# An encoder layer: the FFN's second operand split before it is turned, and three weight blocks visited one sequence at a time

## The chip, the cores and the metric

The kernel runs on one core of a Trainium2 chip. The metric is the device time of one execution in microseconds (us); with several runs, their median. The engines of the core work side by side and in order, each on its own list: TensorE (PE, with its weight loads PEld), VectorE (DVE), ScalarE (ACT), GpSimd (POOL), and SyncE (SP), which issues the DMAs.

## The reference

One encoder layer is applied to two sequences of 1024 positions with 1024 channels, in float32. Cut to what matters:

```python
def encoder_layer(x, ...):
    h = rms_norm(x, norm1)
    proj = h @ w_in                                   # q, k, v, gu, gv
    a = rms_norm(windowed_gqa(q, k, v, ...), attn_out_gain)
    g = rms_norm(chunked_spatial_gating(gu, gv, ...), gmlp_out_gain)
    x = x + jnp.concatenate([a, g], axis=-1) @ w_o    # called x1 below
    h2 = rms_norm(x, norm2)
    return x + (jax.nn.silu(h2 @ w_gate) * (h2 @ w_up)) @ w_down   # D_FF = 2816
```

`rms_norm(x, g)` is `x * rsqrt(mean(x*x) + 1e-6) * g` over the channels.

## The kernel before, in words

Positions are cut into 16 tiles of 128, tiles 0 to 7 for the first sequence (s = 0) and 8 to 15 for the second (s = 1). The kernel goes through these stages: input projections and attention, the gating branch, the output projection with the residual (which gives x1), the gate and up products of the FFN, and the down product.

**Precision.** Every float32 operand of a large product is split into two f16 parts, `hi` (a rounded copy, made by ACT) and `lo` (the rest, made by DVE). A product is then three f16 matmuls into the same PSUM tile: hi by hi, hi by lo, lo by hi.

**Seven products instead of eight.** From the output projection on, a matrix product is done by 2 x 2 blocks with seven block products. Both operands need some sums and differences of their blocks first (four on each side), and the outputs need a few additions behind.

**The FFN's matrices.** Gate and up have 22 column blocks of 128; two of them form a weight block `p`, so there are 11. One "matrix" is the gate (m = 0) or up (m = 1) product of one weight block with one sequence: `matrix(n)` issues seven products of 4 x 3 matmuls of 128x512 (`product`, lines 1895 to 1905). The weights stand still in TensorE (`op`), the sequence's normalised x1 streams past (`tops[s, i]`, seven operands `i`, each with its hi and lo). Between the products `prep(i)` works ahead: it loads the raw weights of the next matrices (`load_raw`), takes their sum of squares (`key_sum`, `key_scale`, which has a small matmul on line 1840) and splits the seven weight operands (`prep_comb`, `prep_hi`, `prep_lo`, lines 1856 to 1886). The list `visits` says which weight block is prepared when and for which sequences; prepared once, it serves all sequences of that visit:

```python
visits = [(0, (0,))] + [(p, (0, 1)) for p in range(1, NP)] + [(0, (1,))]
```

So block 0 is prepared twice, blocks 1 to 10 once, in 12 visits; with gate and up and the sequences there are 44 matrices.

**How the second operand is made.** Behind each pair of position tiles of the output projection, `x1_norm` stores x1, takes the sum of squares (`x1_sq`, ACT) and scales it in place (`x1_scale`, ACT, line 1715). `h2_turn` (line 1723) turns the tile by eight 128x128 transposes on TensorE into PSUM; `h2_out` (line 1730, ACT, eight copies) brings them back with norm2's gain as a scale per partition. `h2_comb` (lines 1751 to 1757, DVE) makes the four block combinations. For s = 0 four of the seven operands are split at once (`part_hi`, `part_lo`, lines 1797 and 1802); everything else is stored in float32 to the scratch tensors `t_d`, loaded again (`top_load`) and split in halves of 128x1024 (`top_hi`, `top_lo`, lines 1783 and 1788), for s = 1 between the products of the first matrices (`top_step`).

**What sets the order.** The part from the first load to the preparation of the first weight block is written as steps in a list `steps`. The table `WHEN` holds a number for each step, by its function's name and count; `plan_order` sorts by it, and the sorted list is the order on every engine. All DMAs are issued from SP, in that same order, so a DMA that waits for its data holds up all DMAs behind it. From the first FFN matrix on, instructions stand in the order in which the functions call them.

**The start.** `warm_mm` runs eight matmuls on zeros while the first weights are on their way.

**On-chip memory.** Work tiles of 4 KB per partition come from pools with a fixed number of slots: L 12, M 8, XL 3, XN 3, S 9.

Of the kernel before, what the change touches and what calls it, by code (L numbers as in the profile page):

```python
# [16 lines left out]
P = 128  # L17
# [3 lines left out]
TS = 8  # L21
# [29 lines left out]
        0,  # L51
    ],
    "warm_mm": [
        62,
    ],
    "x0_load": [
        80, 160, 320, 584, 407, 496, 983, 894,
    ],
    "wq_load": [
        40, 0, 240, 200, 673, 762, 1337, 1482,  # L60
    ],
    "x0_hi": [
        516, 693, 1003, 1269, 1092, 1180, 1679, 1590,
    ],
    "x0_lo": [
        598, 775, 1094, 1351, 1174, 1262, 1792, 1672,
    ],
    "wq_hi": [
        427, 339, 870, 932, 1508, 1446, 2226, 2606,
    ],  # L70
    "wq_lo": [
        520, 431, 963, 1029, 1604, 1539, 2319, 2714,
    ],
    "q0": [
        598, 688, 779, 869, 960, 1103, 1194, 1284, 1375, 1465, 1666, 1757, 1848, 1938, 2082, 2172, 2262, 2380, 2470,
        2560, 2651, 2795, 2965, 3065,
    ],
    "gram": [
        520, 546, 1050, 1077, 2028, 2055, 2353, 2742, 2768, 2781, 2885, 2898, 2912, 2925, 2938, 2952,
    ],  # L80
    "row_load": [
        280, 850,
    ],
    "row_mm": [
        1556,
    ],
    "row_out": [
        1732,
    ],
    "row_store": [  # L90
        1821,
    ],
    "wkv_load": [
        1426, 1570,
    ],
    "wkv_hi": [
        2380, 2300, 2810, 2340, 2667, 2525, 2565, 2851,
    ],
    "wkv_lo": [
        2463, 2385, 2882, 2424, 2780, 2819, 2675, 2922,  # L100
    ],
    "gram_sum": [
        3001,
    ],
    "scale_mm": [
        3055, 7203, 23284, 27506,
    ],
    "scale_add": [
        3102, 7528, 23577, 27552,
    ],  # L110
    "scale_pow": [
        3137, 7584, 23612, 27608,
    ],
    "scale_out": [
        3216, 7664, 23692, 27758,
    ],
    "xn_load": [
        1955, 2088, 1072, 1160, 1249, 4141, 6313, 6903, 8320, 9739, 8574, 11961, 15526, 16895, 20520, 22171,
    ],
    "xn_sum": [  # L120
        2707, 2893, 1812, 1945, 2123, 4685, 6864, 7390, 9651, 12184, 11081, 13532, 16276, 17599, 21121, 22809,
    ],
    "xn_eps": [
        2858, 3037, 2865, 2088, 2267, 4891, 7008, 7556, 9797, 12349, 11290, 13718, 16455, 17742, 21265, 22998,
    ],
    "xn_pow": [
        2893, 3072, 2950, 2123, 2302, 5125, 7108, 7640, 9944, 12384, 11325, 13787, 16490, 17777, 21300, 23032,
    ],
    "kv_mm": [
        3156, 3300, 3730, 3957, 4183, 4327, 3443, 3587, 5853, 6062, 6712, 6860, 8416, 8548, 9722, 9854, 12936, 13111,  # L130
        14723, 14984, 15788, 15946, 17320, 17782, 19792, 19923, 22049, 22192, 24192, 24722, 26585, 26716,
    ],
    "q_out": [
        3307, 3192, 3250, 3966, 6460, 8204, 9248, 11570, 12703, 15642, 17702, 18943, 21842, 23660, 25252, 26508,
    ],
    "v_gain": [
        3341, 4036, 3347, 4332,
    ],
    "k_out": [
        3691, 4166, 4558, 4216, 6238, 7720, 8864, 10390, 13304, 15166, 16113, 18110, 20224, 22359, 25188, 27522,  # L140
    ],
    "v_hi": [
        3818, 4191, 4532, 4467, 6967, 7042, 8715, 10021, 13971, 15151, 16128, 17961, 20096, 22374, 24949, 26884,
    ],
    "v_lo": [
        3944, 4260, 4650, 4578, 7015, 7088, 9132, 10074, 14022, 15197, 16727, 18757, 20255, 22518, 25087, 27026,
    ],
    "qk_sq": [
        3756, 4241, 4623, 4303, 6666, 8323, 9517, 11726, 13350, 15720, 18048, 20298, 21949, 24146, 25329, 27635,
    ],  # L150
    "qk_sum": [
        3849, 4338, 4796, 5018, 6774, 8445, 9609, 11832, 13453, 15812, 18209, 20391, 22042, 24243, 25422, 27820,
    ],
    "qk_pow": [
        4667, 4462, 4920, 5181, 6903, 8574, 9739, 11961, 13582, 15942, 18338, 20520, 22171, 24372, 25551, 27949,
    ],
    "qk_scale": [
        4898, 4723, 5160, 5491, 7175, 8811, 10001, 12275, 13841, 16287, 18593, 20748, 22399, 24600, 25779, 28589,
    ],
    "k_turn": [  # L160
        5328, 5087, 5262, 6701, 7277, 9350, 10517, 14310, 13943, 17451, 19502, 22181, 24323, 26891, 28153, 29807,
# [175 lines left out]
        10357,  # L337
    ],
    "vg_load": [
        120,  # L340
    ],
    "ws_sum": [
        16966,
# [2229 lines left out]
```

## Time and profile before

| | |
|---|---|
| median of 3 runs | 1814.62 us (1811.51 to 1817.87) |
| profiled execution, its own time | 1818.09 us |
| its span, from first to last instruction | 1815.8 us |
| mean granted clock of TensorE | 0.995 |
| instructions in the span | 26756 |
| moved by DMA | 298.87 MB, mean 165 GB/s |
| first FFN matmul on line 1900 | 601.8 us after the span's start |
| first down matmul on line 2410 | 1408.9 us |

How to read it: busy time is the time in which an engine had an instruction running; durations hold the latency at an instruction's end, which the next one may overlap. "Idle before, releaser" is the time in which the engine stood before an instruction, and whose end let it go on. The granted clock is the share of full speed that TensorE was given. The DMA share is the mean busy share of the core's 16 DMA engines.

### The profile page before, as it was taken

Reading aid. Unit: us, or ns where it says so; the run is one execution under the profiler, and the core shown is the slowest. Engines: PE = TensorE matmul, PEld = TensorE weight load, DVE = VectorE, ACT = ScalarE, POOL = GpSimd, SP = SyncE. Lnnn points to the kernel's source line nnn. Section 1 sums busy time; section 2 is a strip of 40 time slices with the busy share of each in tenths; the row PEclk is TensorE's granted clock in tenths of the full one; section 3 lists DMA queues with packets and bytes.
Section 4 is the critical chain, followed back from the end, with each engine's and each line's share of the span. In section 5 each row is a group of like instructions: output and inputs, shape, how many; then the busy total and the mean of one; then the engine's idle time right before and its main releaser. Section 6 shows DMA issues by size and latency. Waiting matters only on the chain.

```text
span 1815.8 us, 26756 instructions
## 1 busy us (share of the span) xinstructions
PE 1789.0 (99%) x10046; PEld 880.8 (49%) x10046; DVE 1167.5 (64%) x2180; ACT 1015.0 (56%) x1951; POOL 113.1 (6%) x142
## 2 busy tenths in 40 slices
PE   9899999999999999999999999999999999999999
PEld 7555554554555444444444444444444444444444
DVE  5887577699888886455564564555647846645651
ACT  6887678897878856344453453434534453333340
POOL 1221120031000000000000000000000000000000
PEclk9999999999999999999999999999999999999999
DMA  8599999987767863232331331323353754333641
GB/s 263 146 224 216 236 257 236 263 274 246 243 215 223 287 218 124 76 122 86 117 122 41 122 115 65 111 77 115 111 203 112 270 175 147 87 115 105 231 140 47
DMA packets 247469, 298.87 MB, mean 165 GB/s; under 512 B 136835, under 2 KB 163459, under 8 KB 247340
## 3 DMA queue, kind: packets, MB, share of 16 engines
q1 hardware_dynamic: 247340, 297.17, 54.0%
q8 instruction: 78, 1.28, 0.3%
q14 instruction: 51, 0.42, 0.1%
HBM read 175.46 MB, written 90.19 MB: 146 GB/s over the span
## 4 chain that ended last, share of the span: by engine, by line
PE 84%; DVE 6%; DMA 4%; ACT 3%; issue 2%; POOL 0%; SPq 0%; POOLq 0%; DVEq 0%; ACTq 0%
PE pd L2410 7%; PE pd L2412 7%; PE pd L2411 7%; PE pa L1900 4%; PE pa L1902 4%; PE pa L1901 4%; PE pd L1900 4%; PE pd L1901 4%; PE pd L1902 4%; PE pc L1900 4%; PE pc L1902 4%; PE pc L1901 4%; PE pb L1900 2%; PE pb L1901 2%; PE pb L1902 2%
## 5 line engine op out<-in xcount | busy, mean ns | idle before, releaser
L2410 PE MATMUL pd<-wop,a 128*128 128x512 f16 x616 | 234.2, 380 | 2.1 <-ACT a L718 2.1
L2411 PE MATMUL pd<-wop,a 128*128 128x512 f16 x616 | 234.1, 380 | 0.0
L2412 PE MATMUL pd<-wop,a 128*128 128x512 f16 x616 | 233.9, 380 | 0.0
L1900 PEld LDWEIGHTS <-op 128*128 128x128 f16 x1232 | 122.3, 99 | 142.8
L1902 PEld LDWEIGHTS <-op 128*128 128x128 f16 x1232 | 120.5, 98 | 145.4
L1901 PEld LDWEIGHTS <-op 128*128 128x128 f16 x1232 | 120.5, 98 | 145.5 <-issue 3.4
L1900 PE MATMUL pa<-top,op 128*128 128x512 f16 x352 | 133.4, 379 | 1.3 <-ACT ua L2018 1.2
L1902 PE MATMUL pa<-top,op 128*128 128x512 f16 x352 | 133.4, 379 | 0.0
L1901 PE MATMUL pa<-top,op 128*128 128x512 f16 x352 | 133.4, 379 | 0.0
L718 ACT ACTIVATE wop<-wd,wdr_r 128x512 f16<-128x512 f32 x66 | 47.3, 720 | 152.5 <-PE pd L2412 148.5
L718 ACT ACTIVATE a<-as,asr_r 128x512 f16<-128x512 f32 x154 | 102.0, 709 | 35.6 <-DMA as<-act_d 16.2
L2029 ACT COPY ub<-pc 128x512 f32<-128x512 f32 x44 | 25.7, 585 | 161.0 <-PE pc L1902 161.0
L719 DVE SCALAR_TENSOR_TENSOR a<-as,asr_r,a 128x512 f16<-128x512 f32 x154 | 109.2, 747 | 9.5 <-ACT a L718 9.5
L719 DVE SCALAR_TENSOR_TENSOR wop<-wd,wdr_r,wop 128x512 f16<-128x512 f32 x66 | 49.2, 749 | 98.8 <-ACT wop L718 98.8
L2410 PEld LDWEIGHTS <-a 128*128 128x128 f16 x616 | 60.5, 98 | 75.4 <-ACT a L718 2.6
L2412 PEld LDWEIGHTS <-a 128*128 128x128 f16 x616 | 60.4, 98 | 73.5 <-issue 0.8
L2411 PEld LDWEIGHTS <-a 128*128 128x128 f16 x616 | 60.4, 98 | 72.7 <-issue 0.8
L1828 ACT ACTIVATE junk_e<-g 128x1024 f32<-128x1024 f32 x44 | 46.4, 1054 | 72.4 <-DVE g L2013 72.3
L1277 ACT ACTIVATE sc<-sc,mx 128x384 f32<-128x384 f32 (+1 forms) x128 | 74.3, 582 | 17.8 <-DVE mx L1261 17.5
L2035 DVE TENSOR_TENSOR ub<-ub,ua 128x512 f32<-128x512 f32 x44 | 30.5, 692 | 82.5 <-ACT ub L2029 82.5
L2010 ACT ACTIVATE g<-g,rs 128x512 f32<-128x512 f32 x57 | 41.1, 722 | 62.5 <-DVE g L2045 35.5
L1261 DVE CUSTOM_DVE_ANT_0 sc<-ps,bias 128x384 f32<-128x384 f32 (+1 forms) x128 | 62.2, 518 | 21.4 <-PE ps L1250 15.4
(413 smaller groups left out, 4417.4 us busy)
## 6 DMA issues: line engine op xcount, KB each, us to landing
as<-act_d SPq DMA_DIRECT2D x77, 512.0 KB, 3.7
act_d<-g SPq DMA_DIRECT2D x66, 256.0 KB, 2.0
raw<-in_wg_dram SPq DMA_DIRECT2D x24, 512.0 KB, 4.0
raw<-in_wu_dram SPq DMA_DIRECT2D x24, 512.0 KB, 4.5
act_d<-sa SPq DMA_DIRECT2D x44, 256.0 KB, 2.6
act_d<-sb SPq DMA_DIRECT2D x44, 256.0 KB, 2.2
wds<-in_wd_dram SPq DMA_DIRECT2D x22, 512.0 KB, 3.9
wd<-in_wd_dram SPq DMA_DIRECT2D x22, 512.0 KB, 5.4
```

Of the source, the lines that this page charges most:

```text
L718: nc.scalar.mul(hi, src, gain)
L719: nc.vector.scalar_tensor_tensor(lo, src, gain, hi, ALU.mult, ALU.subtract)
L1261: nc.vector.tensor_tensor_reduce(out=T["sc", t, hp][:, v, :W], in0=T["ps", t, hp][v][:, :W], in1=bias[:, h, off : off + W], scale=1.0, sca ...
L1277: nc.scalar.activation(sc, sc, AF.Exp, bias=T["mn", t][:, h : h + 1], scale=-1.0, accum_out=T["sum", t][:, h : h + 1])
L1828: nc.scalar.activation(junk_e[0], src, AF.Square, accum_out=acc)
L1900: nc.tensor.matmul(ps, op[:, 0, k, :], th[:, k, :], start=first and k == 0, stop=False, **more)
L1901: nc.tensor.matmul(ps, op[:, 0, k, :], tl[:, k, :], start=False, stop=False, **more)
L1902: nc.tensor.matmul(ps, op[:, 1, k, :], th[:, k, :], start=False, stop=last and k == 3, **more)
L2010: nc.scalar.activation(dst, src, AF.Silu, scale=iv)
L2410: nc.tensor.matmul(ps, a[:, 0, s, cs], wop[:, 0], start=first and n == 0, stop=False, **kw)
L2411: nc.tensor.matmul(ps, a[:, 0, s, cs], wop[:, 1], start=False, stop=False, **kw)
L2412: nc.tensor.matmul(ps, a[:, 1, s, cs], wop[:, 0], start=False, stop=end, **kw)
```

## The change: what it does

- **Operand of the FFN.** norm2's gain is loaded as a row to all partitions (`n2_load`), and `x1_scale` multiplies by both the tile's scale and that row, on DVE. The block combinations (`h2_comb`), `hi` and `lo` are made in the natural layout, positions on partitions. Then the f16 parts are turned by DMA transposes on SP: for s = 0 operands 0 to 3 straight from the chip's memory (`h2_turn`), operands 4 to 6 by way of scratch tensors `nat_d` (`h2_store`, `top_turn`). The TensorE transposes, `h2_out`, `part_hi`, `part_lo`, `t_d`, `top_load`, `top_hi`, `top_lo` are gone.
- **Second sequence.** Only x1 is stored in the projection stage. It is read again, scaled, combined, split and turned during the first eight matrices (the list `late_list`).
- **Visits.** Blocks 0, 1, 2 first for s = 0 alone, blocks 3 to 10 for both, blocks 0, 1, 2 last for s = 1 alone: 14 visits.
- **Order.** The first eight matrices (`FIRST = 8`) become steps of the ordered list, cut in half products (`d_product` and its companions). `WHEN` has new numbers for all steps, also for those ahead of the FFN. In `matrix(n)`, for the rest, some additions and outputs stand later, and the last two outputs and the stores come behind the first product of the next matrix.
- **Start and memory.** Fourteen warm matmuls instead of eight; one small ACT copy is put right at the start; slots XL 4, XN 4, S 11, with the scratch for dynamic DMAs set to 256.
- Down's `blocks` follow the order of the visits with s = 1, so blocks 3 to 10 come ahead of 0, 1, 2.

The diff, cut to its core:

```diff
-    slots = {"L": 12, "M": 8, "XL": 3, "XN": 3, "S": 9}
+    slots = {"L": 12, "M": 8, "XL": 4, "XN": 4, "S": 11}
...
+    early = cp.tile([P, 1], F32, name="early")
+    nc.scalar.copy(early, nhalf[:, 0:1])
...
-        for _ in range(8):
+        for _ in range(14):
             nc.tensor.matmul(ps, T["warm"][:, 0:P], T["warm"], start=True, stop=True)
...
+    def n2_load():
+        T["n2row"] = k4("XL", "n2row")
+        nc.sync.dma_start(T["n2row"], n2.to_broadcast([P, D]))
...
     def x1_scale(t):
-        nc.scalar.mul(T["x1", t], T["xr", t], T["r1", t])
+        nc.vector.scalar_tensor_tensor(T["x1", t], T["xr", t], T["r1", t], T["n2row"], ALU.mult, ALU.mult)
-    def h2_turn(t, z):
-        pt = T["ph2", t, z] = xx(f"ph{t}_{z}", [P, 4, P])
-        for j in range(4):
-            k = z * 4 + j
-            nc.tensor.transpose(pt[:, j, :], T["x1", t][:, k * P : (k + 1) * P], ident)
...
+    def h2_comb(t, i):
+        a, b = {4: (3, 0), 3: (6, 3), 1: (6, 4), 5: (2, 1)}[i]
+        nc.vector.tensor_sub(h2_block(t, i), h2_block(t, a), h2_block(t, b))
+    def h2_hi(t, i):
+        nc.scalar.copy(h2_pack(t, i // 2)[:, i % 2, 0], h2_block(t, i))
+    def h2_lo(t, i):
+        pk = h2_pack(t, i // 2)[:, i % 2]
+        nc.vector.tensor_sub(pk[:, 1], h2_block(t, i), pk[:, 0])
+    def h2_store(t, j):
+        s, cs = h2_cs(t)
+        n = 1 if j == 3 else 2
+        store(nat_d[s][j][cs, 0:n], h2_pack(t, j)[:, 0:n])
+    def h2_turn(t, j):
...
+        dst = T["top16", s, j].rearrange("p i z k c -> p (i z k) c")[:, :, cs]
+        load(dst, h2_pack(t, j).rearrange("p i z d -> p (i z d)"), transpose=True)
+    def top_turn(s, i, z):
+        load(top_pair(s, i)[z], nat_d[s][i // 2][:, i % 2, z], transpose=True)
+    LATE = (0, 2, 6, 4, 3, 1, 5)
+    def late_load(t):
+        T["x1", t] = k4("XL" if t % TS < 4 else "XN", f"xl{t}")
+        load(T["x1", t], x1_d[t])
+    def late_scale(t):
+        nc.vector.scalar_tensor_tensor(T["x1", t], T["x1", t], T["r1", t], T["n2row"], ALU.mult, ALU.mult)
...
+    def late_turn(t, i):
+        pk = late_pack(t, i)
+        s, cs = h2_cs(t)
+        pair = top_pair(s, i)
+        if i < 4:
+            dst = T["top16", s, i // 2][:, i % 2].rearrange("p z k c -> p (z k) c")[:, :, cs]
+            load(dst, pk.rearrange("p z d -> p (z d)"), transpose=True)
+        else:
+            for z in range(2):
+                load(pair[z][:, :, cs], pk[:, z], transpose=True)
...
-    visits = [(0, (0,))] + [(p, (0, 1)) for p in range(1, NP)] + [(0, (1,))]
+    visits = [(p, (0,)) for p in range(3)] + [(p, (0, 1)) for p in range(3, NP)] + [(p, (1,)) for p in range(3)]
...
+    def late_list():
+        for t in range(TS, TS + 4):
+            for u in (t, t + 4):
+                yield (late_load, u)
+            for u in (t, t + 4):
+                yield (late_scale, u)
+            for i in LATE:
...
+                for fn in (late_hi, late_lo, late_turn):
+                    yield (fn, t, i)
...
+    for n in range(FIRST):
+        v, m, s = mats[n]
+        last_one = v == FIRST // 2 - 1
+        for i in range(7):
+            for part in range(2):
+                add(d_product, n, i, part)
...
+            key = (v, 1) if m == 0 else (v + 1, 0)
+            if not (m and last_one):
...
+                add(prep_hi, key, i)
+                add(prep_lo, key, i)
+            upto = len(late) * (7 * n + i + 1) // (7 * FIRST)
+            for fn, *args in late[nlate:upto]:
+                add(fn, *args)
...
-    for n in range(len(mats)):
+    for n in range(FIRST, len(mats)):
         matrix(n)
```

More of the change, by code (lines that the diff above doesn't have):

```diff
@@ L659 @@
+    "key_sum": [
+        61103, 61770, 64440, 64693, 67963,
+    ],
+    "key_mm": [
+        61372, 62030, 64777, 65046,
+    ],
+    "key_add": [
+        61419, 62107, 64874, 65094,
+    ],
+    "key_pow": [
+        61481, 62169, 64935, 65156,
+    ],
+    "key_out": [
+        61577, 62321, 65087, 65374,
     ],
@@ L686 @@
     vg: bass.AP,
+    n2: bass.AP,
     tab: bass.AP,
@@ L769 @@
     x1_d = [dr.tile([P, D], F32, name=f"x1_d{t}") for t in range(NT)]
-    t_d = [[dr.tile([P, 4, 512], F32, name=f"t_d{s}_{i}") for i in range(7)] for s in range(2)]
+    nat_d = [[dr.tile([512, 2 - j // 3, 2, 512], F16, name=f"nat_d{s}_{j}") for j in range(4)] for s in range(1)]
     act_d = [dr.tile([P, NF // 2, 2, 512], F32, name=f"act_d{i}") for i in range(7)]
@@ L2018, in matrix @@
         nc.scalar.copy(u2, pa)
+        while behind:
+            behind.pop(0)()
         prep(0)
@@ new lines, in d_pre, with d_product @@
+    def d_pre(n, q):
+        if mats[n][1] == 0 and q:
+            return d_out(n, q)
+        return (d_bank(n, "a"), d_tile(n, "a")[:, 1], d_tile(n, "b")[:, 0], d_tile(n, "a")[:, 0])[q]
+    def d_product(n, i, part):
+        key, s, _ = d_info(n)
+        op = wops[key, i]
+        th, tl = tops[s, i]
+        ps = d_bank(n, "abacdcd"[i])
+        first, final = i in (0, 1, 3, 4), part == 1
+        for k in (2 * part, 2 * part + 1):
+            more = dict(skip_group_check=not first)
+            nc.tensor.matmul(ps, op[:, 0, k, :], th[:, k, :], start=first and k == 0, stop=False, **more)
+            nc.tensor.matmul(ps, op[:, 0, k, :], tl[:, k, :], start=False, stop=False, **more)
+            nc.tensor.matmul(ps, op[:, 1, k, :], th[:, k, :], start=False, stop=final and k == 3, **more)
@@ new lines, in d_store, with key_mm @@
+    def d_store(n, i):
+        _, s, p = d_info(n)
+        sa, sb = (T.get(("ds", n, c)) for c in range(2))
+        if i in (0, 2, 5):
+            a = d_out(n, {0: 0, 2: 1, 5: 2}[i])
+        else:
+            a = {1: lambda: sa[:, 1], 3: lambda: sb[:, 0], 4: lambda: sa[:, 0], 6: lambda: sb[:, 1]}[i]()
+        store(act_d[i][:, p, s, :], a)
+    def key_mm(key):
+        T["kp", key] = xx(f"pk{key[0]}_{key[1]}", [P, 2])
+        nc.tensor.matmul(T["kp", key], onec, wsc[key], start=True, stop=True)
@@ new lines, in key_add, with key_pow, key_out @@
+    def key_add(key):
+        tot = small("m", 1)
+        nc.vector.tensor_reduce(tot, T["kp", key], AX.X, ALU.add)
+        e = T["ke", key] = small("den", 2)
+        for j in range(2):
+            nc.vector.tensor_scalar(e[:, j : j + 1], tot, W_NORM**-2, 1e-37, ALU.mult, ALU.add)
+    def key_pow(key):
+        r = T["kr", key] = small(("f", "sums")[key[1]], 2)
+        nc.gpsimd.tensor_tensor(r, T["ke", key], pm, ALU.pow)
+        wsc[key] = r[:, 0:1]
+    def key_out(key):
+        iv = winvs[key] = small(("rs", "v_ms")[key[1]], 1)
+        nc.vector.tensor_mul(iv, T["kr", key][:, 1:2], n2r[:, 1:2])
```

774 lines of the change are left out of this document (419 added, 355 removed), and 179 rows, old and new, of the table WHEN.

## The prediction

> **What bounds the kernel now.** I read first the page's busy times, then its chain of waits, then TensorE's own waits, and last the busy times by stage. The page (busy us, share of the span, instructions) and the engines' shares of the chain that ended last:
>
> ```profile
> PE 1789.0 (99%) x10046; PEld 880.8 (49%) x10046; DVE 1167.5 (64%) x2180; ACT 1015.0 (56%) x1951; POOL 113.1 (6%) x142
> PE 84%; DVE 6%; DMA 4%; ACT 3%; issue 2%; POOL 0%; SPq 0%; POOLq 0%; DVEq 0%; ACTq 0%
> ```
>
> TensorE is busy for 99% of the span and is 84% of the chain. So a matmul taken away is worth its slot, and other engines matter only where TensorE comes to wait for them. The stages (us from:to, length, then busy us and instructions of PE, PEld, DVE, ACT, POOL; then granted clock, DMA share, GB/s):
>
> ```profile
> 0.00:446.20 446.20, 429.32 (x3624) 248.31 (x3625) 333.81 (x839) 354.69 (x804) 83.33 (x100) 0.98 0.92 234
> 446.20:601.70 155.50, 154.76 (x818) 82.99 (x816) 130.87 (x225) 124.47 (x270) 11.65 (x17) 1.00 0.71 234
> 601.70:746.70 145.00, 141.86 (x665) 65.09 (x663) 105.13 (x157) 89.85 (x152) 3.12 (x4) 1.00 0.58 192
> 746.70:891.70 145.00, 145.00 (x679) 66.38 (x678) 78.90 (x133) 66.34 (x112) 2.78 (x4) 1.00 0.29 102
> ```
>
> The second row is the bulk of the output projection, the third as long a stretch as eight FFN matrices take, the fourth the FFN in its steady state. TensorE stands idle 446.2 - 429.3 = 16.9 us before the projection, 0.7 in it, 3.1 in the first FFN stretch, and not at all in the next.
>
> **The transposes that go.** The change takes all TensorE transposes of the normalised x1 out (line 1723). First the groups by line (count, busy us, mean ns, idle before), then four rows of TensorE in order of time (start, us; in brackets the idle before and what ended it):
>
> ```profile
> L1723 PE MATMUL ph<-ident,xs 128*128 128x128 f32 x128 | 18.1, 274 | 1.9 <-ACT xs L1715 1.9
> L1840 PE MATMUL pks<-mx,onec 128*128 128x2 f32 x40 | 5.6, 209 | 0.0
> ```
>
> ```profile
> 463.33 0.38 PE L1665 MATMUL wc<-wo5h,mo 128*128 128x512 f16 x1
> 463.55 0.60 PE L1723 MATMUL ph<-ident,xs 128*128 128x128 f32 x4
> 463.98 0.38 PE L1663 MATMUL wc<-wo5h,mo 128*128 128x512 f16 x1
> ...
> 607.96 2.13 PE L1723 MATMUL ph<-ident,xs 128*128 128x128 f32 x16 [1.48 <-ACT xs L1715]
> ```
>
> The group's 18.1 us counts the latency at the end of each set. What four transposes cost the engine is start to start: 463.98 - 463.55 = 0.43 us, where a 128x512 matmul takes 463.55 - 463.33 = 0.22. So 32 sets x 0.43 = **13.8 us** leave TensorE, 28 of the 32 in the projection, where it never rests and nothing else can hide them. Their 1.9 us of waits for line 1715 go too: no TensorE instruction of the projection waits for the scaled tile any more. **-15.7 us**.
>
> **Two extra visits.** Weight blocks 0, 1 and 2 are prepared twice, before only block 0: 14 visits instead of 12, four more prepared matrices. On TensorE that is the scale sum of line 1840: 20 matrices cost 5.6 us, four more **+1.1 us**. Their 4 MB of loads, 28 splits on each of ACT and DVE, and 16 sums lie beside matmuls; the fourth stage row has DVE at 78.9 and ACT at 66.3 of 145 us. The late single-sequence visits double the preparation per matmul, still under both engines' room; I cost them at nothing there. Without the cover, one matrix's preparation is some 7 us of DVE.
>
> **The start.** Rows of time from the first 10 us, then three stretches of it:
>
> ```profile
> 1.19 3.19 PE L832 MATMUL ps_warm<-warm 128*128 128x512 f16 x8 [1.19 <-DVE warm L827]
> 3.95 1.28 ACT L856 ACT_TABLE_LOAD   x1 [3.95 <-DMA wqr<-in_w_in_dram]
> 6.63 1.43 PE L904 MATMUL gram<-wqt 128*128 128x128 f32 x8 [2.25 <-ACT wqt L856]
> ```
>
> ```profile
> 6.00:8.00 2.00, 1.37 (x9) 1.38 (x10) 1.85 (x3) 1.19 (x2) 0.00 (x0) 0.81 0.91 244
> 8.00:10.00 2.00, 2.00 (x6) 1.61 (x6) 0.30 (x2) 0.72 (x2) 0.00 (x0) 0.50 1.08 353
> 10.00:14.00 4.00, 4.00 (x19) 3.23 (x18) 2.86 (x7) 2.98 (x5) 0.82 (x2) 0.92 1.12 314
> ```
>
> The table load of ACT waits behind the first weights; the new first copy of ACT brings it ahead of them, up to 1.28 us earlier. After the 2.25 us of idle the granted clock falls to 0.50, which costs 0.4 + 1.0 + 0.3 = 1.7 us over these rows. Six more warm matmuls (6 x 0.22 to 6 x 0.40 us) end at about 6 us, so the hole closes. Against a gain of 3.0 stands that the DMA share is already 0.9 to 1.1 here, so later loads may swallow it: bounds 0 and 3.0, I take the middle, **-1.5 us**. [...]
>
> **VectorE in the projection and in the first eight matrices.** The second operand is now split before it is turned, so the subtractions become 56 of 128x512, with 16 scalings of 128x1024, for what now are 16 + 20 splits and 16 ACT scalings. DVE's rows in order of time show what an instruction costs when it is fed:
>
> ```profile
> 617.13 0.69 DVE L1863 TENSOR_TENSOR ss<-raw 128x512 f32<-128x512 f32 x1
> 617.73 0.69 DVE L2023 TENSOR_TENSOR ua<-pb,ua 128x512 f32<-128x512 f32 x1
> ...
> 638.22 0.75 DVE L1886 SCALAR_TENSOR_TENSOR op<-ss,es_er,op 128x512 f16<-128x512 f32 x1
> 638.88 0.75 DVE L1886 SCALAR_TENSOR_TENSOR op<-st,es_er,op 128x512 f16<-128x512 f32 x1
> ...
> 647.53 1.22 DVE L1788 TENSOR_TENSOR top<-tr,top 128x1024 f16<-128x1024 f32 x1
> 648.66 0.69 DVE L2054 TENSOR_TENSOR sa<-g,g 128x512 f32<-128x512 f32 x1
> ```
>
> Start to start 0.60, 0.66 and 1.13 us, less than the durations beside them. A 128x1024 scaling is not in the trace: between 1.13 and 2 x 0.66; I take 1.24, the 1.13 raised by 0.66/0.60. Eight matrices are 672 matmuls x 0.2156 (145.0 us in the fourth stage row holds 8 x 84 of them and the sums) = 144.9 us of TensorE. DVE's work in them: 40 sums x 0.60 + 16 products x 0.66 + 16 output sums x 0.60 + seven weight matrices (49 splits x 0.66 + 28 sums x 0.60) + the late operand (8 x 1.24 + 16 x 0.60 + 28 x 0.60) = 24.0 + 10.6 + 9.6 + 49.1 + 36.3 = 130 us, 90% of the time. By listed durations it would be 147, more than there is. The present stretch holds 105.1 us of DVE and loses 3.1 us of TensorE, 1.5 of them (607.96) in the waits already taken out above. I let the new one lose 4, which is **+2.4 us** over the 1.6 left; bounds -1.6 (no waits) and, by the durations, 147 - 145 + 4 - 1.6 = +4.4.
>
> In the projection DVE loses about 39 rows of 0.69 us and gets 8 scalings and 44 rows: 130.9 - 27 + 41 = 145 listed us against 155.5 - 12.2 = 143.3 of TensorE, by starts (0.60/0.69) about 126. It fits by the starts. ACT loses the 128 copies of line 1730 and the scalings of 1715, so DVE waits less for it. I add nothing here; the other answer is a rival below.
>
> **DMA and SP's queue.** Rows of SP in order of time; issues with the median us to landing; and the one queue in the attention stage (60 to 340 us) and in the steady FFN (packets, MB, share):
>
> ```profile
> 96.90 3.41 SPq L977 DMA_TRANSPOSE xh<-xq  x1
> 102.53 0.34 SPq L980 DMA_DIRECT2D xh_d<-xh  x1
> ```
>
> ```profile
> tr<-t_d SPq DMA_DIRECT2D x20, 512.0 KB, 5.2
> t_d<-hf SPq DMA_DIRECT2D x16, 256.0 KB, 3.2
> t_d<-ta SPq DMA_DIRECT2D x12, 256.0 KB, 3.9
> t_d<-tb SPq DMA_DIRECT2D x12, 256.0 KB, 3.9
> pT<-ph SPq DMA_TRANSPOSE x64, 4.4
> xh<-xq SPq DMA_TRANSPOSE x16, 5.7
> ```
>
> ```profile
> DMA packets 126739, 63.80 MB, mean 228 GB/s; under 512 B 115730, under 2 KB 115730, under 8 KB 126707
> q1 hardware_dynamic: 126707, 63.38, 98.6%
> ```
>
> ```profile
> q1 hardware_dynamic: 6048, 14.68, 28.2%
> ```
>
> The steady queue moves 14.68 MB in 28.2% of 145 us, 359 GB/s. In the attention stage the small packets, 115730 x 256 B = 29.6 MB, are the transposes; the other 33.8 MB take 94 of 276 us, so the transposes run at 163 GB/s, 3.2 us for 512 KB. The change turns 14.7 MB (8 + 6 of 512 KB for the first sequence, 28 blocks of 256 KB for the second): 90 us of DMA. The traffic through t_d goes, 20 x 512 + 40 x 256 KB, 58 us. With the packed stores, x1 read again and four weight matrices that is some 65 us more in about 290 us where 0.71 x 155 + 0.58 x 145 = 194 are used: near 90%, below the attention stage's. SP holds 3.41 us for 2048 columns, so the late 28 blocks take about 48 us of its 145, with some 54 plain issues at 0.34 another 18. Behind a turn that waits for its split stand the next weights and the stores on SP, for which ACT and DVE wait next; behind a late scaling that waits for x1 stand the next matrix's splits on DVE, and TensorE waits for those. I cost this at nothing, covered by the matrices; bare, one turn is 5.7 us. [...]
>
> **Sum.** -15.7 + 1.1 - 1.5 + 2.4 = -13.7 us. The order list of the whole front part is new as well; its 16.9 us of idle can shrink or grow. A quarter of it either way, 4 us, I allow in the forecast's own range; in the sum I take nothing. The profiled execution took 1818.09 us, its span 1815.8, so 2.3 us lie around it; the runs' median is 1814.62. 1818.1 - 13.7 = 1804.4 for the profiled one, and **1801 us** for the median.
>
> **Rivals.** (a) *The list also removes waits.* Nothing of the change needs the 16.9 us of idle ahead of the projection; if half of it goes and the first eight matrices lose nothing: 1801 - 8 - 4 = 1789. For it: the waits are ones of order, a few us each. Against: the attention stage's queue is full at 98.6%. (b) *VectorE takes TensorE's place.* If an instruction costs its listed duration, DVE is at 145 of 143.3 us in the projection and at 147 of 145 in the eight matrices; the 12.2 us taken from TensorE in the projection come back as waits: 1801 + 12 = 1813, no change. Against: the start-to-start rows. For: in the projection DVE now stands 25 us, waiting for others, and hardly any room is left for that. (c) *Slower: the late turns queue one behind another.* The second sequence's first matrix needs every turned block of the late list: 16 whole turns and 24 half ones, 40 instructions on SP in 145 us, 3.6 us each. If each has to land before the next, at a mean of 4.2 us (under the 4.4 and 5.7 above, halves being shorter), the last lands 168 - 145 = 23 us late and TensorE stands for it: 1801 + 23 = 1824. It decides from 3.6 us a turn; for slower it needs 4.1. Against: in the attention stage the transposes ran at the full DMA rate, so they overlap. (d) *The turned operand isn't the saving*: were the 13.8 us hidden now, nothing would come. The matmul rows close up before and behind line 1723, so I leave it no chance.
>
> **How the numbers follow.** A measurement here tells about 0.3%, 5.4 us, from no change. The forecast (1793 to 1809) has 0.55, (a) 0.17, (b) 0.17, (c) 0.11. Faster: 0.55 + 0.17 = 0.72; same 0.17; slower 0.11. The range reaches from (a) to the upper edge of (b): 1788 to 1818; its own part is 1793 to 1809.
>
> **What would show it.** Right: no line like 1723 in the changed profile, and some 14 us less of TensorE between 446 us and the first FFN matmul; a clock of 1.0 from about 6 us on; DVE busy above 90% in the first eight matrices with TensorE idle at most 5 us there. Wrong: TensorE waiting for a product's DVE split, or for a turned tile by DMA at the first matrix of the second sequence; more than 25 us of idle before the projection.

## The result and the profile after

| | before | after |
|---|---|---|
| median of 4 runs | 1816.24 us (1811.51 to 1818.72) | 1786.03 us (1784.81 to 1788.25) |
| profiled execution, its span | 1818.09 us, 1815.8 | 1785.38 us, 1783.6 |
| mean granted clock | 0.995 | 0.999 |

The ratio is 0.9838, interval 0.9814 to 0.9862: 30 us faster, where 13.7 were forecast. The way was right, the size not, and 1786 lies just outside the range of 1788 to 1818.

The page of after, busy times and the engines' shares of the chain:

```profile
PE 1766.6 (99%) x9932; PEld 866.1 (49%) x9932; DVE 1214.5 (68%) x2276; ACT 993.1 (56%) x1874; POOL 125.7 (7%) x146
PE 88%; DVE 4%; ACT 3%; DMA 3%; issue 1%; POOL 1%; SPq 0%; DVEq 0%; ACTq 0%; POOLq 0%
```

The stages of after (from:to, length, busy us and instructions of PE, PEld, DVE, ACT, POOL, granted clock, DMA share, GB/s): before the projection's bulk, that bulk, the first eight matrices, eight matrices of the steady FFN.

```profile
0.00:440.00 440.00, 427.40 (x3625) 248.57 (x3626) 339.54 (x842) 360.34 (x816) 86.91 (x98) 1.00 0.96 246
440.00:578.70 138.70, 138.12 (x711) 69.33 (x710) 130.79 (x224) 81.71 (x150) 13.84 (x16) 1.00 0.79 240
578.70:723.70 145.00, 145.00 (x678) 66.14 (x676) 132.37 (x222) 89.91 (x153) 8.56 (x9) 1.00 0.81 197
723.70:868.70 145.00, 145.00 (x679) 66.39 (x678) 80.76 (x135) 67.23 (x114) 2.78 (x4) 1.00 0.34 118
```

The first eight matrices, where a loss was allowed for, lose nothing: TensorE is busy for all 145.00 us. The projection's bulk loses 0.6 us. DVE is the closest second, busy for 94% of the projection's bulk and 91% of the eight matrices.

Two stretches of before, in the same columns, show what the prediction had no term for: the attention stage's first part, and the start of the down product.

```profile
36.00:130.00 94.00, 89.35 (x703) 54.12 (x702) 79.24 (x209) 80.72 (x193) 22.51 (x18) 0.96 0.73 185
1400.00:1430.00 30.00, 27.92 (x123) 12.19 (x122) 26.38 (x47) 13.11 (x21) 1.07 (x1) 0.94 0.68 239
```

The same two in after:

```profile
36.00:130.00 94.00, 93.69 (x746) 59.90 (x745) 83.20 (x214) 87.36 (x202) 24.07 (x21) 1.00 0.91 213
1400.00:1430.00 30.00, 30.00 (x141) 13.62 (x140) 26.02 (x40) 20.26 (x32) 0.00 (x0) 1.00 0.84 292
```

In the first, before lost 94 - 89.35 = 4.65 us of idle and 0.04 x 94 = 3.8 us of clock, after 0.3 in all. Added up over the span, idle of TensorE went from 26.8 to 17.0 us (-9.8, span less busy time) and time lost to the clock (1 less the clock, times the span) from 9.1 to 1.8 us (-7.3); the transposes' slots are another 13.8 (32 x 0.43). The span fell by 32.2 us, so by this account the waits and the lost clock, 17.1, are more than the transposes' slots. It says where time was lost, not what each part of the change is worth alone; that is what the experiments ask.

From the first matmul of the projection to the first one of the FFN, before and then after:

```profile
417.60:601.80 184.20, 180.42 (x1011) 96.75 (x1008) 158.64 (x277) 147.72 (x312) 15.82 (x23) 1.00 0.70 232
417.90:578.80 160.90, 159.36 (x840) 79.81 (x837) 152.84 (x266) 99.71 (x187) 20.42 (x20) 1.00 0.79 246
```

This stretch alone became 23 us shorter, and the projection starts no earlier. So the new front does not bring the projection forward; it puts more of TensorE's work ahead of it (171 instructions fewer stand here: the 112 transposes, and some 60 that now run in the front). The FFN up to the first down matmul (now at 1380.5) gave 5.4 us, the rest of the kernel 3.8.

### The profile page after: what moved, and what is told of

The parts are those of the page before. It is cut to its first block, busy times and chain, and to the rows that moved or that the text cites. A ratio compares the mean times of both kernels' runs of the same rounds, so it can differ in the third digit from the quotient of the medians.

```text
span 1783.6 us, 26545 instructions
## 1 busy us (share of the span) xinstructions
PE 1766.6 (99%) x9932; PEld 866.1 (49%) x9932; DVE 1214.5 (68%) x2276; ACT 993.1 (56%) x1874; POOL 125.7 (7%) x146
## 4 chain that ended last, share of the span: by engine, by line
PE 88%; DVE 4%; ACT 3%; DMA 3%; issue 1%; POOL 1%; SPq 0%; DVEq 0%; ACTq 0%; POOLq 0%
PE pd L2635 7%; PE pd L2633 7%; PE pd L2634 7%; PE pd L1965 3%; PE pd L1966 3%; PE pc L1966 3%; PE pa L1966 3%; PE pc L1965 3%; PE pa L1967 3%; PE pa L1965 3%; PE pc L1967 3%; PE pd L1967 3%; PE pb L1965 2%; PE pb L1966 2%; PE pb L1967 2%; PE ps L1316 1%
## 5 line engine op out<-in xcount | busy, mean ns | idle before, releaser
L1965 PEld LDWEIGHTS <-op 128*128 128x128 f16 x1008 | 100.3, 100 | 116.5
L1967 PEld LDWEIGHTS <-op 128*128 128x128 f16 x1008 | 98.6, 98 | 119.0
L1966 PEld LDWEIGHTS <-op 128*128 128x128 f16 x1008 | 98.5, 98 | 116.5
L2064 ACT COPY ub<-pc 128x512 f32<-128x512 f32 x36 | 21.1, 586 | 164.4 <-PE pc L1967 164.4
L1965 PE MATMUL pa<-top,op 128*128 128x512 f16 x288 | 109.2, 379 | 0.0
L1966 PE MATMUL pa<-top,op 128*128 128x512 f16 x288 | 109.2, 379 | 0.0
L1967 PE MATMUL pa<-top,op 128*128 128x512 f16 x288 | 109.2, 379 | 0.0
L1368 DVE TENSOR_TENSOR ph<-sc,ph 128x768 f16<-128x768 f32 (+1 forms) x64 | 56.3, 888 | 18.1 <-ACT ph L1363 17.5
```

The costliest lines, as they stand in the source:

```text
L1368: nc.vector.tensor_sub(ph[:, 1], T["sc", t, hp][:, :, :W], ph[:, 0])
L1965: nc.tensor.matmul(ps, op[:, 0, k, :], th[:, k, :], start=first and k == 0, stop=False, **more)
L1966: nc.tensor.matmul(ps, op[:, 0, k, :], tl[:, k, :], start=False, stop=False, **more)
L1967: nc.tensor.matmul(ps, op[:, 1, k, :], th[:, k, :], start=False, stop=last and k == 3, **more)
```

## The experiments

Three theories on where the unforecast half came from were tested beside the forecast's own steps. *Slots*: the deeper buffers. *Seam*: before, ACT and DVE were nearly as full as TensorE where the projection meets the FFN (198 and 216 of 260 us busy at 440:700, TensorE 256), and the change relieves them. *Order*: the new numbers of the front. A gain in us with a minus sign is (ratio - 1) x 1816; by it the change is worth -29.4. Differences from after ("above after") are those of the medians; by the ratios some come out up to 3 us otherwise (e8: 9.8 instead of 12.7), and each time carries an interval of some 2 to 5 us either way.

**e1: the transposes put back as extra work.** Each transpose of the mixed rows in the projection is issued twice, 128 more.

```diff
-            nc.tensor.transpose(pt[:, c, :], T["mix", t][:, k * P : (k + 1) * P], ident)
+            for _ in range(2):
+                nc.tensor.transpose(pt[:, c, :], T["mix", t][:, k * P : (k + 1) * P], ident)
```

> The changed kernel, but each TensorE transpose of the output projection's first operand is issued twice into the same place: 128 extra 128x128 transposes of the same form as those that the change took away, in the same stage. If a transpose costs its slot (0.43 us for four), 13.9 us more than the changed kernel's 1786, so 1800. If taking them away was worth more than the slot (18 us by the group's busy time, or 23 us, what the front lost altogether), 1804 to 1809.

1801.26 us, ratio 0.992 (0.9891 to 0.995): 15.2 us above after. In the new arrangement 128 transposes cost their slots, and a little clock (idle is 16.4 us where after has 17.0; the clock is 0.998 against 0.999).

**e2: the transposes taken out of before.**

```diff
     def h2_turn(t, z):
-        pt = T["ph2", t, z] = xx(f"ph{t}_{z}", [P, 4, P])
-        for j in range(4):
-            k = z * 4 + j
-            nc.tensor.transpose(pt[:, j, :], T["x1", t][:, k * P : (k + 1) * P], ident)
+        pass
...
-            nc.scalar.mul(T["hf", t][:, k, :], T["ph2", t, z][:, j, :], n2s[:, k : k + 1])
+            nc.scalar.mul(T["hf", t][:, k, :], T["x1", t][:, k * P : (k + 1) * P], n2s[:, k : k + 1])
```

> The kernel before without its 128 TensorE transposes of x1: the eight scaled copies per tile read x1 from on-chip memory in its natural layout, so the second operand of the FFN is not turned and the output is another; nothing else is left out, and the order list is the old one. By the forecast's term -13.8 us of slots and up to -1.9 us of waits against the kernel before: 1800 to 1803. If the transposes also held up ACT, DVE and the projection's other work, 1793 or less.

1813.76 us, 0.9989 (0.9974 to 1.0004): 2 us, hardly to be told from nothing. The same 128 transposes that cost 15 us in after were nearly free in before. The stretch 440:700 us, first of before, then of e2:

```profile
440.00:700.00 260.00, 256.12 (x1294) 129.84 (x1293) 215.98 (x350) 198.08 (x394) 14.99 (x21) 1.00 0.70 231
```

```profile
440.00:700.00 260.00, 247.72 (x1170) 116.23 (x1169) 215.39 (x348) 201.06 (x393) 15.94 (x21) 0.98 0.68 229
```

Idle rose from 3.9 to 12.3 us, and the clock fell to 0.98 (5 us). TensorE's waits of e2 in this stretch (line waited for: us in total, times, longest):

```profile
PE pd L1898 <- DVE top_4l L1785: 3.0, 1, 3.0
PE pa L1897 <- ACT ua L2015: 2.3, 2, 1.8
PE pd L1897 <- ACT ub L2030: 1.8, 1, 1.8
PE wa L1665 <- DVE mo L1638: 1.6, 2, 0.9
PE wb L1663 <- DVE xr L1696: 1.2, 1, 1.2
```

The freed slots became waits (8.4 us more; 11.3 of the 12.3 are for ACT and DVE) and lost clock (5).

**e9: the slots alone**, in before.

```diff
-    slots = {"L": 12, "M": 8, "XL": 3, "XN": 3, "S": 9}
+    slots = {"L": 12, "M": 8, "XL": 4, "XN": 4, "S": 11}
...
-    nc = _bacc.Bacc("TRN2", target_bir_lowering=False, num_devices=1)
+    nc = _bacc.Bacc("TRN2", target_bir_lowering=False, num_devices=1, dynamic_dma_scratch_size=256)
```

> The kernel before with the new numbers of slots (XL 4, XN 4, S 11) and the smaller scratch, nothing else. In the profile of before the first activation of the down stage comes late: 2.08 us of TensorE idle at 1419 us and half clock behind it, about 3.8 us together; in the profile of after, and in that of before with the new front numbers and the new slots, it is gone. Theory 'slots': it goes here too, about 1812.5 us (1811 to 1814), and the window 1400:1430 shows clock 1.00. Rival 'chance of the order': it stays, 1815 to 1818.

1810.32 us, 0.9967 (0.9952 to 0.9982): -6.0 us. First before (TensorE's rows in order of time, start and us, in brackets the idle and what ended it), then the stretch 1400:1430 of e9:

```profile
1416.56 0.38 PE L2412 MATMUL pd<-wop,a 128*128 128x512 f16 x1
1419.02 0.39 PE L2410 MATMUL pd<-wop,a 128*128 128x512 f16 x1 [2.08 <-ACT a L718]
...
1420.54 0.63 PE L2410 MATMUL pd<-wop,a 128*128 128x512 f16 x1
1420.97 0.63 PE L2411 MATMUL pd<-wop,a 128*128 128x512 f16 x1
...
1423.53 0.51 PE L2411 MATMUL pd<-wop,a 128*128 128x512 f16 x1
1423.87 0.38 PE L2412 MATMUL pd<-wop,a 128*128 128x512 f16 x1
```

```profile
1400.00:1430.00 30.00, 30.00 (x142) 13.58 (x141) 28.32 (x49) 14.95 (x25) 1.08 (x1) 1.00 0.84 294
```

The down product prepares four (`LEAD`) activation tiles ahead, each in an XL slot until both sequences are split. With the three slots of before the fourth load goes out at 1419.78 us, behind 5.1 us of SP's waiting for a split on DVE, after the second sequence's scale (POOL, 1417.13 to 1418.20), for which ACT's split waited 4.4 us; with the four of after it goes out with the third at 1335.00. The wait and some eight matmuls at 0.43 us behind it (8 x 0.21) were 2.1 + 1.7 = 3.8 us; the other 2 us lie within the spread of the runs. The slots of XN and S and the scratch were changed along with XL and not taken apart.

**e10 and e11: the new visits in before**, without and with the removal of e2, slots as in e9. `prep` is that of after; the second sequence's 28 load and split steps go at half the pace.

```diff
-    visits = [(0, (0,))] + [(p, (0, 1)) for p in range(1, NP)] + [(0, (1,))]
+    visits = [(p, (0,)) for p in range(3)] + [(p, (0, 1)) for p in range(3, NP)] + [(p, (1,)) for p in range(3)]
...
         def prep(i):
+            if n < 8 and (7 * n + i) % 2 == 0:
+                top_step()
```

> The kernel before with the new slots and the new 14 visits; the second sequence's operand is still turned on TensorE, stored in float32, loaded and split, but its 28 load and split steps go at half the pace, over the first eight matrices. The list of the front is unchanged. Theory 'seam' (ACT and DVE share the limit where the projection meets the FFN, since both split operands and weights there): the first FFN matrices are relieved, -2 to -5 us of waits, +1.1 for four more key sums: 1811 to 1815. Theory 'list' (only the ordered first eight matrices and the new front numbers bring the rest): 1815 to 1818.

> As the one with the new visits, and without the 128 transposes on TensorE (the operand is copied from the normalised x1 as it lies, so it is not turned; everything else as there). Taken out of the kernel before, the transposes brought 2 us. Theory 'seam': with the splitting spread over eight matrices they are no longer covered in the FFN, and most of the 13.8 us comes through: 11 to 14 us under the run with the new visits alone, about 1801. Theory 'list': again 2 to 4 us under it. In between (5 to 10): the waits inside the projection itself (where the operand's copies and splits are unchanged) keep the rest.

e10: 1815.97 us, 1.0 (0.9985 to 1.0015), slower than the slots alone. In its profiled execution (1809.97 us, the fastest of its runs) TensorE's longest wait is for the squares of a key sum on ACT.

```profile
PE pks L1840 <- ACT junk_e L1828: 4.6, 3, 3.9
```

e11: 1812.08 us, 0.9981 (0.9971 to 0.999), 4 us under e10. Both are what theory 'list' of their expectations says (only the ordered first eight matrices and the new front bring the rest) and not what 'seam' says: spreading the second sequence out does not uncover the transposes.

**e13, e14 and e15: ACT's copies.** The change also removes ACT's 128 copies behind the transposes (line 1730). e13 takes both out of before, slots as in e9; e14 adds the visits; e15 puts as many copies into after.

```diff
     def h2_out(t, z):
-        if ("hf", t) not in T:
-            T["hf", t] = k4("L", f"hf{t}", (P, KD, P))
-        for j in range(4):
-            k = z * 4 + j
-            nc.scalar.mul(T["hf", t][:, k, :], T["ph2", t, z][:, j, :], n2s[:, k : k + 1])
+        T["hf", t] = T["x1", t].rearrange("p (k c) -> p k c", c=P)
```

```diff
         ms = T["ms1", t] = small("x_ms", 1)
+        for k in range(KD):
+            nc.scalar.copy(xs[:, k * P : (k + 1) * P], T["xr", t][:, k * P : (k + 1) * P])
         nc.scalar.activation(xs, T["xr", t], AF.Square, scale=1.0 / 32.0, accum_out=ms)
```

> The kernel before with the new slots, without the 128 transposes on TensorE and without ACT's 128 copies behind them: the sums and splits read the normalised x1 as it lies, not turned and without norm2's gain. The new slots alone took 5.6 us off. Theory 'ACT': the copies (29 us of ACT in the 184 us from the first to the last matmul of the projection) kept the splits of the projection's own operand late, and TensorE waited; without them the 13.8 us come through: 1797 (1794 to 1800), 500:620 of the windows with under 3 us of idle. Rival 'splits of the FFN operand': what keeps TensorE waiting is DVE's sums and splits of both sequences' operand and of the weights at the seam, which stay: 1804 to 1810.

> The same with the new visits as well, the second sequence's loads and splits at half the pace over the first eight matrices. With the transposes alone taken out these visits gave 1812. Theory 'ACT': as without the visits, 1797 to 1802. Rival 'splits of the FFN operand': the visits make room for them, so this one is 5 to 10 us faster than the run without the visits, and near 1800; that one is not.

> The kernel after with 128 more copies of 128x128 on ACT, eight ahead of each tile's sum of squares (into the tile that the squares overwrite), some 30 us of ACT in the projection, where ACT is busy 99.8 of 160.9 us. Theory 'ACT': TensorE waits for it again, +8 us or more (1794 and up). Rival: ACT has room in the new projection, within 3 us of 1786.

e13: 1802.78 us, 0.9921 (0.9904 to 0.9939), -14.3, of which the slots are -6.0: transposes and copies together bring 8.4 where the transposes alone brought 2. The time lies between the numbers of theory 'ACT' (to 1800) and of its rival (from 1804). e14: 1807.19 us, 0.9943 (0.9927 to 0.9959), above what either theory says; against e11 the copies are 6.9 us, and the visits cost again. Both runs also free the slots that `hf` held in the pool L, which was not taken apart from the copies. e15: 1799.0 us, 0.9902 (0.9886 to 0.9919), 13 us above after. The copies of e15 from 419 to 592 us (count, busy us, mean ns, idle before), its longest wait and its projection (of after: 140.00, 139.42 busy):

```profile
L1777 ACT COPY xs<-xr 128x128 f32<-128x128 f32 x109 | 23.4, 295 | 5.6 <-DVE xr L1766 3.3 <-issue 2.1
```

```profile
PE wd L1733 <- ACT sc L1747: 6.0, 2, 4.2
```

```profile
440.00:580.00 140.00, 132.42 (x668) 65.10 (x667) 122.16 (x206) 92.44 (x233) 12.10 (x15) 0.99 0.72 221
```

ACT is busy for only 92 of 140 us there, and yet 23.4 us of copies cost 13: they stand in ACT's order ahead of the emptying of `wd`, for which TensorE waits. The two waits for it are 6.0 of the 8.7 us by which idle grew; the lost clock grew by another 3.6. So theory 'ACT', that the copies keep TensorE waiting, holds in after; in before it is about half of the 11.8 us that e2 was short of the slots.

**e8: DVE's room in the first eight matrices.** The 28 late subtractions are issued twice, 28 x 0.60 = 16.8 us more DVE.

```diff
-        nc.vector.tensor_sub(pk[:, 1], h2_block(t, i), pk[:, 0])
+        for _ in range(2):
+            nc.vector.tensor_sub(pk[:, 1], h2_block(t, i), pk[:, 0])
```

> The changed kernel with each of the 28 late DVE subtractions of the second sequence issued twice: 28 x 0.60 = 16.8 us more of DVE in the first eight matrices. Counted by starts DVE would be at 130 + 17 = 147 of 145 us, so TensorE has to wait 3 to 10 us: 1789 to 1796. If DVE had still room (its present instructions fit with much idle left), no change. If DVE was at its bound already, all 17 us: 1803.

1798.73 us, 0.9892 (0.9875 to 0.9908): 12.7 us of the 16.8 reach the end, more than the 3 to 10 expected, so some 4 us of room were there (7 by the ratios). The eight matrices' stretch of e8:

```profile
578.70:723.70 145.00, 133.96 (x610) 59.62 (x609) 141.31 (x235) 86.17 (x147) 8.56 (x9) 0.99 0.68 175
```

**e3, e4, e12: old and new order lists joined.** e3 gives before (slots as in e9) the numbers of after up to the projection and moves the later ones by 900; e4 and e12 give after the old numbers up to there and move the later ones by 2500 and 800. First e3, then e12; every number ahead of the projection is exchanged like these.

```diff
     "gram": [
-        520, 546, 1050,
+        864, 891, 917,
...
     "o_product": [
-        39868, 40474, 41386,
+        40768, 41374, 42286,
```

```diff
     "gram": [
-        864, 891, 917,
+        520, 546, 1050,
...
     "o_product": [
-        40175, 40564, 41672,
+        40975, 41364, 42472,
```

> The kernel before, with the changed kernel's order numbers for all steps ahead of the output projection and for preparing its weights, the old numbers moved later by 9 us for the projection and what follows, and the changed numbers of slots. TensorE's work is the same. If the unforeseen part of the gain is the order of the front part (idle and the half clock behind it), the clock share goes up from 0.995 and the time goes down by 6 to 11 us against the kernel before: 1805 to 1810. If that part came with the projection or the FFN, no change: 1814 to 1818 (or some us more, for the 9 us by which the projection stands later in the list).

> The changed kernel with the old order numbers for all steps ahead of the output projection (the old start too, but with fourteen warm matmuls), and the changed ones moved later by 8 us from the preparation of the projection's weights on. If the order of the front part carries the unforeseen gain, 6 to 11 us more than the changed kernel: 1792 to 1797, with a granted clock of 0.996 or less. If it doesn't, 1784 to 1788.

> The kernel after with the old numbers for all steps ahead of the output projection (the projection's and the later steps' numbers moved by 800, which stands for 8 us, so that the old front fits ahead of them). Theory 'front list' (the new numbers of the front bring about 8 us less idle and 7 us less clock loss): 1794 to 1798. Rival 'front list is worth nothing by itself' (what is gained ahead is given back at the seam to the projection, as when the new front was put on the kernel before): 1784 to 1789.

e3: 1817.1 us, 1.0007 (0.9994 to 1.002). The kernel that ran as e4 had its later numbers moved by 2500 (25 us), not by the 8 us that its expectation names; its 1826.68 us, 1.0062 (1.0039 to 1.0085), answer nothing, and e12 is the one meant: 1805.41 us, 0.9953 (0.9936 to 0.997), 19 above after. Two stretches of e3 and of e12:

```profile
36.00:130.00 94.00, 93.70 (x749) 60.35 (x749) 82.47 (x211) 87.22 (x202) 23.80 (x21) 1.00 0.88 210
390.00:440.00 50.00, 39.25 (x325) 21.62 (x324) 44.96 (x91) 35.38 (x73) 11.76 (x14) 0.93 0.53 187
```

```profile
36.00:130.00 94.00, 89.40 (x703) 53.83 (x703) 80.66 (x209) 81.81 (x196) 21.82 (x16) 0.96 0.76 189
270.00:440.00 170.00, 151.89 (x1431) 82.63 (x1428) 128.32 (x309) 142.55 (x317) 33.46 (x39) 0.98 0.90 249
```

36:130 follows the list: 93.7 at clock 1.00 with the new numbers, 89.4 at 0.96 with the old. But both lose about as much or more at the joint (idle at 390:440 is 3.9 us in before and 10.8 in e3; at 270:440 it is 7.2 in after and 18.1 in e12), so neither prices it at the end. e12 lies above both of its expected ranges.

**e16, e17, e18: only the first part reordered.** The steps below 15000 (150 us) of after in the order of before (e16, below); those below 20000 of before in the order of after, slots as in e9 (e17); that with the edits of e13 (e18). The part keeps its own numbers, which are dealt out anew to its steps in the other kernel's order; behind it the list is as it was.

```diff
     "gram": [
-        864, 891, 917,
+        749, 750, 1256,
...
     "wkv_load": [
-        926, 837,
+        1604, 1768,
```

> The kernel after; the steps of the first 150 us stand in the order of the kernel before, all later ones as they are. Theory 'front order': the window 36:130 falls from 93.7 busy at clock 1.00 to about 89.4 at 0.96, 8 us, and this goes through to the end, less the 2 to 4 us that the late row load costs the new start: 1790 to 1794. Rival 'given back': the stages behind have waits of their own and swallow it, 1784 to 1788.

> The kernel before with the new slots (1810.3 by itself); the steps of the first 200 us stand in the order of the kernel after. Theory 'front order': window 36:130 at 93.7 busy and clock 1.00, 8 us less, 2 to 4 lost again at the start by the late row load: 1802 to 1806. Rival 'given back': 1808 to 1813.

> As the last, and without the 128 transposes and ACT's 128 copies behind them (the sums and splits read the normalised x1 as it lies, not turned and without norm2's gain); with the old order this took 7.5 us beyond the slots, 1802.8. If the parts add up: 1795 to 1799. What is then left to 1786 is the seam of the projection and the first FFN matrices (560:620 of the windows), which only the new way of making the operand closes. If they do not add up: 1801 to 1804.

e16: 1807.38 us, 0.9953 (0.9936 to 0.997), 21 above after. e17: 1808.78 us, 0.9965 (0.9954 to 0.9975), as the slots alone. e18: 1801.55 us, 0.9916 (0.99 to 0.9933), 1.2 under e13. All three miss the numbers of theory 'front order': e17 and e18 came out where the rival has them (given back; the parts do not add up), e16 above both. Stretches of e16 and of e17:

```profile
36.00:130.00 94.00, 89.30 (x717) 54.20 (x716) 82.97 (x216) 84.08 (x200) 22.37 (x17) 1.00 0.80 192
130.00:200.00 70.00, 61.14 (x518) 33.94 (x516) 40.60 (x104) 41.95 (x100) 9.42 (x8) 0.88 0.87 191
```

```profile
36.00:130.00 94.00, 93.69 (x749) 60.17 (x749) 82.63 (x211) 87.28 (x202) 23.99 (x21) 1.00 0.87 212
200.00:270.00 70.00, 65.98 (x521) 34.45 (x519) 44.76 (x121) 47.91 (x114) 13.31 (x11) 1.00 0.99 227
```

The idle at 36:130 comes and goes with the order in every kernel, and the lower clock (0.96) with it except in e16, which keeps 1.00 there; each time the gain is taken back where the orders meet (e16: 8.9 us of idle and 8.4 of clock at 130:200; e17: 4.0 us at 200:270, and a start with the new list's early `row_load`, of which more below). It seems that the old order behind is fitted to an old front; no run shows that directly. 'Order' is right on the place and unproved on the price.

**e5, e6, e7: small edits of after.** `row_load` behind the first weights; the old places of additions, outputs and stores in `matrix`; eight warm matmuls.

```diff
     "row_load": [
-        118, 1413,
+        1412, 1413,
```

```diff
-        while behind:
-            behind.pop(0)()
...
-        nc.vector.tensor_add(u2, pb, u2)
         prep(1)
+        nc.vector.tensor_add(u2, pb, u2)
         product(key, s, 2, pa, False, True)
+        out_(g0[:, 0], pa)
...
-        behind.append(rest)
```

```diff
-        for _ in range(14):
+        for _ in range(8):
```

> The changed kernel with one number of the order list changed: the load of the bias table, first on SP, is put behind the first weights and inputs (118 to 1412). In the changed kernel's trace SP stands until 4.19 us for that load, which waits for GpSimd to fill its tile, and the first weights go out at 4.59 us instead of 1.18. If the start is on the path, the hole of 2.9 us before the first useful matmul and the half clock behind it go: 3 to 5 us less than the changed kernel, 1781 to 1783. If later loads set the pace of the start, less than 1 us.

> The changed kernel with the old order of additions, outputs and stores in the 36 matrices after the first eight. If this order is what took the 2.1 us wait and the half clock away at the start of the down product, 3 to 4 us more than the changed kernel: 1789 to 1790, with a wait of pd for ACT a. If that went away for another reason (the last visits), no change: 1784 to 1788.

> The changed kernel with eight warm matmuls instead of fourteen. They end ahead of the first weights in either case, so the hole before the first useful matmul grows from 2.9 to some 4.2 us and nothing later moves: 1784 to 1788. If the longer hole keeps the clock low for longer, 1 to 3 us more.

e5: 1781.29 us, 0.9801 (0.9786 to 0.9817), 4.7 under the median of after and the fastest kernel here (one of its four runs, 1785.75, lies among those of after). e6: 1786.12 us, 0.9827 (0.9812 to 0.9842); e7: 1785.06 us, 0.9819 (0.9804 to 0.9834): no change. SP's queue in after, then in e5 (start, us, line, transfer):

```profile
0.74 0.40 SPq L802 DMA_DIRECT2D cst<-in_consts_dram  x1
4.19 0.35 SPq L974 DMA_DIRECT2D tabs<-in_tab_dram  x1
4.59 1.36 SPq L915 DMA_DIRECT2D wqr<-in_w_in_dram  x3
```

```profile
0.74 0.39 SPq L802 DMA_DIRECT2D cst<-in_consts_dram  x1
1.19 1.36 SPq L915 DMA_DIRECT2D wqr<-in_w_in_dram  x3
```

The table of the relative positions is first in the new list, its tile is filled by POOL, and SP holds every load behind it till 4.19 us. In e5 the fourteen warm matmuls last until the first useful one, with no gap:

```profile
5.92 1.87 PE L970 MATMUL gram<-wqt 128*128 128x128 f32 x12
```

Over the first 36 us after has 4.9 us of idle and 1.8 of lost clock, e5 1.2 and none.

## Why the prediction was right in its way and wrong in its size

The sum came to -13.7 us where -29.4 were measured. Its largest term, the transposes, was too large for what it named; two parts that did bring time had no term or 0: the slots (-6.0 by e9), and the waits with the lost clock, which fell by 17.1 us between the two profiles (some 3.8 of it the slots').

**Transposes, -15.7.** The 13.8 us are gone from TensorE, and e1 puts them back at their price. What failed in before, the kernel that it was worked out for, is "28 of the 32 in the projection, where it never rests and nothing else can hide them", and that rival (d) was left "no chance". A TensorE that never rests shows that its slots are full, not that the others have room: ACT and DVE were so close behind (198 and 216 of the 260 us at 440:700) that e2 gained 2 us of the 15.7. Rival (d) was the truth for this edit alone. "ACT loses the 128 copies of line 1730 ... I add nothing here" was the term that mattered: they are worth 6.3 us in the old arrangement (e13 against e2, less the slots' 6.0; the freed L slots are in it) and 13 in the new one (e15).

**Waits and order, 0 +- 4.** The term left the clock out. The idle ahead of the projection went from 16.9 to 12.6 us, 4.3 and so about the quarter that the bound allowed. But its own row had the clock at 0.98 over 446 us, another 7 to 9 us, and 36:130 alone held 3.8 of that beside 4.65 of idle. Rival (a), 1789, was the nearest, and in part by luck: the eight matrices lose nothing, as it says, but half of the idle did not go; the clock and the slots made up the number. What the order is worth alone stays open (e3, e12, e16 to e18).

**Slots.** They are in the list of edits and have no term in the sum: -6.0 us (e9). The row was there, in the stretch 1400:1430, at the far end of the kernel from the change's core.

**The eight matrices, +2.4.** DVE's 130 us by starts, 90%, were right (132.4 busy, the 1024-wide scaling 1.20 us from start to start where 1.24 were worked out); the 4 us of loss were not there, the result is the lower bound, -1.6. e8 shows how near it was: some 4 us of room.

**The start, -1.5.** Wrong in sign. ACT's table load did move ahead, to 0.73 us, but TensorE waits longer than before, by its rows of after in order of time and a stretch of the windows:

```profile
8.76 1.27 PE L970 MATMUL gram<-wqt 128*128 128x128 f32 x8 [2.90 <-ACT wqt L922]
12.00:14.00 2.00, 2.00 (x6) 1.54 (x6) 1.06 (x3) 0.95 (x3) 0.00 (x0) 0.50 1.09 351
```

Not ACT was last but the first weights, 3.4 us later than before (issued at 4.59 against 1.18 us); the diff had `row_load` at 118, ahead of the first `wq_load` at 158. e5 prices the place at 4.7 us. With the weights this late the six more warm matmuls close nothing (e7); in e5 they do close the hole, as the prediction had it. So its sign "a clock of 1.0 from about 6 us on" came in e5 and not in after.

**Key sums, +1.1, and DMA, 0.** Four more sums measure 1.2 us, eight small matmuls on a line of the first eight matrices beside the 40 of before:

```profile
L2458 PE MATMUL pk<-mx,onec 128*128 128x2 f32 x8 | 1.2, 222 | 0.0
```

No TensorE instruction of the late part waits for a turned tile, so (c) did not come. (b) did not either, as its start-to-start rows said.

**What adds up.** Slots -6.0 and transposes with copies -8.4 are measured by edits; 15 of the 29.4 us are not, and no experiment prices them. Between the profiles of e13 and after (spans 1802.2 and 1783.6), by idle and lost clock, they lie at 36:130 and 500:680. The rows of e13, and two of its waits:

```profile
36.00:130.00 94.00, 89.37 (x687) 54.09 (x685) 79.24 (x211) 79.88 (x192) 22.57 (x18) 0.96 0.73 183
500.00:680.00 180.00, 172.48 (x819) 80.97 (x818) 154.17 (x244) 115.64 (x179) 11.14 (x14) 0.99 0.74 244
```

```profile
PE pa L1893 <- ACT op L1875: 2.6, 1, 2.6
PE pb L1893 <- ACT op L1875: 2.0, 1, 2.0
```

That is 8.4 us against 0.3 in after, and 9.3 (7.5 of idle, 1.8 of clock) against none. The idle at the first place follows the order list, but no run that changed the list alone kept the gain. At the second e13 waits for the first weights' splits on ACT; the visits do not cure it (e14). Whether the new way of splitting or the ordered first eight matrices does stays open: neither was tried without the other.

## What to carry to other kernels

Work taken from a full engine paid here only as far as the next engines had room in that very stretch (2 us of 13.8 in e2), and what they lose with it (here 128 small copies, 6.3 us) may be the larger half; take it out alone and see before counting on its slots. A wait can bring slow clock behind it (1.7 us at 1419 in before), so count idle and lost clock together, and read every stretch with a clock under 1.00 as a place to gain. An edit that only deepens buffers, or moves one early DMA that waits for its tile, needs a term of its own (here 6.0 us, e9, and 4.7, e5).

## What the runs showed of the hardware that was not expected

In before, 2.08 us of idle ended at 1419.02; TensorE then started six matmuls at nearly full pace (1419.02 to 1420.25, 0.25 us apart in the mean) and only from about 1420.4 to 1423.8 one each 0.43 us instead of 0.22: the half clock came 1.4 us after the wait was over and lasted 3.4 us. The granted clock was 1.00 at 1419:1420, 0.68 at 1420:1421, 0.50 at 1421:1423, 0.61 at 1423:1424 and 1.00 again at 1424:1425.

How long the wait was does not settle it. In e7 TensorE stood for 3.97 us, and the clock stayed at 1.00 behind it:

```profile
8.75 2.97 PE L970 MATMUL gram<-wqt 128*128 128x128 f32 x12 [3.97 <-ACT wqt L922]
8.75:30.00 21.25, 21.25 (x96) 17.55 (x97) 15.25 (x28) 15.88 (x29) 0.77 (x2) 1.00 1.06 345
```

In after, 2.90 us of the same wait were followed by 0.50 (at 12:14). What decides between the two was not tested.
